# Interleaving the high and low parts of each weight tile in a three-pass float32r matmul kernel

## Chip, cores and metric

One core of one Trainium2 chip runs the whole program. The metric is the device time of one execution in microseconds (us), the median of several runs. The profile is of one execution of its own.

## What is computed

Two layers of a decoder trunk on 512 tokens of width 1024, in float32. Each layer has three sub-layers, each between two RMS norms and with a residual: a mixer (dilated attention heads and mLSTM heads), cross attention into 256 memory tokens, and a gated MLP. Cut to the dense products, which take nearly all of the time:

```
for l in range(DEPTH):                                     # 2
    proj  = rmsnorm(x, pre_mix_g[l]) @ w_in[l]             # 512x1024 @ 1024x3592
    x    += rmsnorm(concat(attn, mlstm) @ w_out[l], ...)   # @ 1024x1024
    q, k, v = rmsnorm(x, pre_mem_g[l]) @ wq, mem @ wk, mem @ wv
    x    += rmsnorm(softmax(q k / 16) v @ wo[l], ...)
    u     = causal_dwconv(rmsnorm(x, pre_ffn_g[l]) @ w_up[l], ...)   # @ 1024x5632
    a, g  = split(u)
    x    += rmsnorm((gelu(g) * a) @ w_down[l], ...)        # 512x2816 @ 2816x1024
```

## The kernel before

**Three products for one.** TensorE gets float32r operands, which keep fewer bits than float32. Each operand is therefore split into a high part (the value rounded to float32r) and a low part (the rest), and `mm3` (L113) issues three matmuls for one: high x high, high x low, low x high. `split` (L98) makes the parts: ACT writes the high part with a cast, DVE subtracts it from the source and writes the low part.

**Units of weights.** All weights lie in DRAM as 134 units per layer of 128 x 1024 values. `load_raw` (L84) brings one into a tile `raw` (two buffers, DMAs on SP's queue), `w_split` (L89) splits it into the tiles `whi` and `wlo` (five buffers each). Each of these has room for 1152 values per partition, of which 1024 are used from an offset of 0 or, with `HALF_OFF`, of 32 values (128 bytes).

**Who moves and who stands.** In a matmul one operand is loaded into the array (stationary, 128 columns) and the other streams through it (moving, up to 512 columns). In the names of the profile the first input is the moving one: pg<-whi,B moves a weight against a stationary activation, pg<-B,whi moves an activation against a stationary weight. `feat_gen` (L169) and `feat_halves` (L180) hold weights stationary, the first with 512 moving columns (or 256 for the memory tokens), the second with 256. `tok_gen` (L197) and `down` (L1218) move the weights, 512 columns at a time. B are tiles of activations, S and T tiles of the MLP's pool `forms`, mem the memory tokens.

**The up projection.** `up_products` (L1059) forms seven products of 256 moving columns for each pair of units j, from sums and differences of weight blocks and of activations. POOL builds the sums in tiles T (L1101 to L1104), `high` (L1111) casts on ACT and `low` (L1123) subtracts, on DVE for the kinds a, t and u (1024 values), on POOL for kind b (512 values, a tile of its own with 1120 values).

**Order.** PE's instructions stand in the order in which the program issues them, with side tasks woven in by a table of times (`PACE`, `tick`). In the up projection that holds for ACT, DVE, POOL and SP as well. Elsewhere a scheduler orders these four, from the tiles' dependences and buffers.

## Time and profile before

| | |
|---|---|
| median of 3 runs | 1577.69 us (1576.15 to 1578.36) |
| the profiled execution | 1576.06 us, of it the span 1574.3 us |
| PE busy (matmul) | 1547.4 us, 98% of the span, 9480 matmuls |
| PEld busy (weight load) | 1371.0 us, 87% |
| DVE busy | 1049.2 us, 67% |
| ACT busy | 892.0 us, 57% |
| POOL busy | 326.5 us, 21% |
| DMA | 173.13 MB, mean 110 GB/s |

Matmuls overlap: the busy time of one reaches from its start to its modelled end, and the next starts before that. How long a matmul holds the engine is therefore read from the distance of two starts, not from its busy time. A group's idle time is that of the engine just before its instructions.

### The profile page before, as it was taken

To read this page: it belongs to the slowest core of one execution; us is meant where nothing else is said; L and a number is where in the kernel's file an instruction comes from. 1 tells how busy PE (TensorE), PEld (TensorE's weight loads), DVE (VectorE), ACT (ScalarE), POOL (GpSimd) and SP (SyncE) were. 2 spreads that over 40 slices of the span, in tenths; PEclk is the share of its full clock that TensorE was granted. 3 is DMA by queue.
4 is the path that set the end of the run, shared out by engine and by line. 5 is a ranking of instruction groups with operands and counts; after the bars stand their busy time and mean duration, and the time that the engine had idled before them with its cause. 6 is when DMAs were issued, how large, how long until landed. Compare 5 with 4: busy or idle time off the path is not lost.

```text
span 1574.3 us, 24497 instructions
## 1 busy us (share of the span) xinstructions
PE 1547.4 (98%) x9480; PEld 1371.0 (87%) x9480; DVE 1049.2 (67%) x1808; ACT 892.0 (57%) x1578; POOL 326.5 (21%) x292
## 2 busy tenths in 40 slices
PE   7999999999999999999999999999999999999998
PEld 5788888998899999988887888889888899999886
DVE  5687646746597777763376886557566977777433
ACT  5677574545466666653257775745445666666321
POOL 0000110100026666600010002101000466663000
PEclk9999999999999999999999999999999999999999
DMA  5421244552242333332333223445411233332331
GB/s 177 129 94 62 92 137 153 155 187 94 68 136 95 108 108 108 108 121 94 108 95 107 94 74 94 137 144 161 161 54 42 96 108 108 108 114 82 127 102 58
DMA packets 55430, 173.13 MB, mean 110 GB/s; under 512 B 6801, under 2 KB 9617, under 8 KB 55314
## 3 DMA queue, kind: packets, MB, share of 16 engines
q1 hardware_dynamic: 55314, 171.57, 33.4%
q8 instruction: 74, 1.21, 0.3%
q14 instruction: 42, 0.34, 0.1%
HBM read 165.22 MB, written 6.33 MB: 109 GB/s over the span
## 4 chain that ended last, share of the span: by engine, by line
PE 82%; DVE 6%; DMA 5%; ACT 3%; issue 2%; POOL 1%; SPq 0%; POOLq 0%; DVEq 0%; ACTq 0%
PE pg L107 51%; PE pa L107 28%; PE pa L111 2%; DMA raw<-in_w_dram 2%; DVE wlo L100 1%; DMA raw<-in_memt_dram 1%; ACT whi L99 1%; DVE xg L256 1%; POOL sm L230 1%; ACT junk L235 1%; DVE x L369 1%; DMA raw<-dk 1%; DVE wlo L1126 1%; DMA raw<-dv 1%; DMA dk<-kf 0%
## 5 line engine op out<-in xcount | busy, mean ns | idle before, releaser
L107 PE MATMUL pg<-B,whi 128*128 128x256 f32 (+1 forms) x1800 | 420.7, 327 | 8.2 <-DVE ql L995 3.9
L100 DVE TENSOR_TENSOR wlo<-raw,whi 128x1024 fp32r<-128x1024 f32 x188 | 230.6, 1228 | 215.7 <-ACT whi L99 213.1
L99 ACT CAST whi<-raw 128x1024 fp32r<-128x1024 f32 x188 | 197.2, 1050 | 217.8 <-PE pg L107 139.7
L107 PEld LDWEIGHTS pg<-B,whi 128*128 128x128 f32 x1800 | 290.8, 189 | 28.3 <-DVE ql L995 4.3
L107 PE MATMUL pg<-whi,B 128*128 128x512 f32 x896 | 297.8, 399 | 0.0
L107 PE MATMUL pg<-B,wlo 128*128 128x256 f32 (+1 forms) x896 | 288.4, 322 | 0.0
L107 PEld LDWEIGHTS pg<-whi,B 128*128 128x128 f32 x896 | 168.6, 188 | 35.1 <-DVE B L100 1.3
L230 POOL TENSOR_TENSOR sm<-sm,mhalf 128x1 f32<-128x1 f32 x56 | 34.3, 612 | 724.2 <-DVE sm L355 548.3
L107 PEld LDWEIGHTS pg<-B,wlo 128*128 128x128 f32 x896 | 168.9, 188 | 13.6
L107 PE MATMUL pg<-wlo,B 128*128 128x512 f32 x448 | 175.3, 391 | 0.6 <-DVE sm L248 0.6
L107 PE MATMUL pa<-S,whi 128*128 128x256 f32 x960 | 175.5, 283 | 0.0
L1031 DVE SCALAR_TENSOR_TENSOR u<-pg,fcw,u 128x511 f32<-128x511 f32 (+1 forms) x176 | 131.3, 747 | 38.2 <-ACT u L1026 35.2
L107 PEld LDWEIGHTS pa<-S,whi 128*128 128x128 f32 x960 | 148.4, 190 | 0.0
L107 PE MATMUL pa<-S,wlo 128*128 128x256 f32 x480 | 135.6, 282 | 0.0
L1126 DVE TENSOR_TENSOR wlo<-T,whi 128x1024 fp32r<-128x1024 f32 x80 | 103.9, 1299 | 9.7 <-ACT whi L1120 9.7
L107 PE MATMUL pa<-whi,S 128*128 128x512 f32 x320 | 105.9, 390 | 0.0
L107 PE MATMUL pg<-whi,S 128*128 128x512 f32 x320 | 105.4, 390 | 0.0
L1120 ACT CAST whi<-T 128x1024 fp32r<-128x1024 f32 x80 | 83.5, 1044 | 32.9 <-PE pg L107 30.8
L1026 ACT ACTIVATE u<-pg,fcw 128x512 f32<-128x512 f32 x88 | 68.5, 779 | 57.2 <-PE pg L107 37.2
L107 PEld LDWEIGHTS pg<-wlo,B 128*128 128x128 f32 x448 | 84.7, 189 | 15.8 <-DVE wlo L100 1.0
L107 PEld LDWEIGHTS pa<-S,wlo 128*128 128x128 f32 x480 | 90.9, 189 | 0.0
L1126 POOL TENSOR_TENSOR b<-rg,b 128x512 fp32r<-128x512 f32 x40 | 51.6, 1290 | 142.7 <-ACT b L1120 142.7
(264 smaller groups left out, 2942.5 us busy)
## 6 DMA issues: line engine op xcount, KB each, us to landing
raw<-in_w_dram SPq DMA_DIRECT2D x228, 512.0 KB, 3.5
rg<-in_w_dram SPq DMA_DIRECT2D x40, 512.0 KB, 3.5
gain<-in_gains_dram SPq DMA_DIRECT2D x11, 512.0 KB, 4.0
raw<-in_memt_dram SPq DMA_DIRECT2D x20, 256.0 KB, 3.0
tb<-tb_d SPq DMA_DIRECT2D x16, 256.0 KB, 3.5
x<-in_x_dram SPq DMA_DIRECT2D x8, 256.0 KB, 5.6
e<-nmu_d SPq DMA_DIRECT2D x8, 256.0 KB, 3.7
dv<-vf SPq DMA_DIRECT2D x8, 256.0 KB, 4.4
```

What stands on the lines that cost most here:

```text
L99: ACT.copy(hi, src)
L100: DVE.tensor_sub(lo, src, hi.bitcast(F32))
L107: PE.matmul(o, lhs, rhs, **kw)
L111: PE.transpose(o, src, idn)
L230: POOL.tensor_tensor(r, v, mhalf[:, :1], ALU.pow)
L235: ACT.activation(junk[:, :src.shape[-1]], src, AF.Square, accum_out=s_)
L256: DVE.scalar_tensor_tensor(xg, xt[:, c], r, g[h], ALU.mult, ALU.mult)
L369: DVE.scalar_tensor_tensor(xs[t][:, cc], self.hg[hh, t], r, xs[t][:, cc], ALU.mult, ALU.add)
L1026: ACT.activation(u, acc, AF.Identity, bias=fcw_t[:, m, 3:4], scale=fcw_t[:, m, 2:3])
L1031: DVE.scalar_tensor_tensor(u[:, q:], acc[:, :512 - q], fcw_t[:, m, 2 - q:3 - q], u[:, q:], ALU.mult, ALU.add)
L1120: ACT.copy(ws[j, kind][0], source(j, kind))
L1126: sub(ws[j, kind][1], source(j, kind), ws[j, kind][0].bitcast(F32), ALU.subtract)
```

## The change

Each weight unit now has one tile `wi` of 128 x 1036 x 2 values in place of `whi` and `wlo`. Its high part is every even value, its low part every odd one, so two neighbouring columns of either part lie 8 bytes apart. The tile of kind b is interleaved in the same way, without offset. The 12 unused pairs make the pitch of the five buffers 8288 bytes, which is 16 x 512 + 96; the offsets `off` and `HALF_OFF` are gone. The pool of weights is 4640 bytes per partition smaller, and what is allocated after it lies that much lower. A reader of the names should know that whi, wlo and b's parts are all called wi or b in the changed kernel.

```diff
-    def w_split(raw, off=0):
-        hi = pp.tile([128, 1152], F32R, tag="whi", name=nm("whi"), bufs=5)[:, off:off + 1024]
-        lo = pp.tile([128, 1152], F32R, tag="wlo", name=nm("wlo"), bufs=5)[:, off:off + 1024]
+    def w_tile():
+        both = pp.tile([128, 1036, 2], F32R, tag="wi", name=nm("wi"), bufs=5)
+        return both[:, :1024, 0], both[:, :1024, 1]
+
+    def w_split(raw):
+        hi, lo = w_tile()
         split(raw, hi, lo)
         return hi, lo
 
-    def load_unit(l, i, off=0):
-        return w_split(load_raw(l, i), off)
+    def load_unit(l, i):
+        return w_split(load_raw(l, i))
...
-    HALF_OFF = 32
...
     def feat_halves(l, units, act, dones, between):
-        ws = [load_unit(l, u, HALF_OFF) for u in units]
+        ws = [load_unit(l, u) for u in units]
...
             if kind == "b":
-                t = forms.pool.tile([128, 1120], F32R, tag="b", name=nm("b"))
-                ws[j, kind] = t[:, 96:608], t[:, 608:1120]
+                t = forms.pool.tile([128, 512, 2], F32R, tag="b", name=nm("b"))
+                ws[j, kind] = t[:, :, 0], t[:, :, 1]
             else:
-                ws[j, kind] = [pp.tile([128, 1152], F32R, tag=tg, name=nm(tg), bufs=5)[:, HALF_OFF:HALF_OFF + 1024]
-                               for tg in ("whi", "wlo")]
+                ws[j, kind] = w_tile()
             ACT.copy(ws[j, kind][0], source(j, kind))
```

PE's and POOL's instructions keep their order. On ACT and DVE the scheduler puts 21 of the 308 casts of weights one to three places later, and the subtracts with them. One place on ACT, early in the first layer's mixer, where the casts of weights (raw is the source) stand among the casts of the attention's keys (kh). Before:

```order
L99 CAST whi_941<-raw_939 128x1024
L733 CAST kh_436<-pg_505 64x512
L734 CAST kh_436<-pg_505 64x512
L733 CAST kh_437<-pg_505 64x512
L734 CAST kh_437<-pg_505 64x512
L649 ACT_TABLE_LOAD
```

And with the change:

```order
L735 CAST kh_432<-pg_499 64x512
L736 CAST kh_432<-pg_499 64x512
L102 CAST wi_931<-raw_929 128x1024
L735 CAST kh_433<-pg_499 64x512
L736 CAST kh_433<-pg_499 64x512
L651 ACT_TABLE_LOAD
```

The cast of the weight moved behind the first two casts of keys. On DVE at the same place, where the weights' low parts stand among those of the queries (qa) and keys (kl). Before:

```order
L100 TENSOR_TENSOR wlo_808<-raw_805,whi_807 128x1024
L726 SCALAR_TENSOR_TENSOR qa_434<-pg_444,qa_434 64x512
L726 SCALAR_TENSOR_TENSOR qa_435<-pg_444,qa_435 64x512
L100 TENSOR_TENSOR wlo_942<-raw_939,whi_941 128x1024
L735 TENSOR_TENSOR kl_428<-pg_505,kh_436 64x512
L735 TENSOR_TENSOR kl_429<-pg_505,kh_437 64x512
```

And with the change:

```order
L728 SCALAR_TENSOR_TENSOR qa_430<-pg_439,qa_430 64x512
L103 TENSOR_TENSOR wi_798<-raw_796,wi_798 128x1024
L728 SCALAR_TENSOR_TENSOR qa_431<-pg_439,qa_431 64x512
L737 TENSOR_TENSOR kl_424<-pg_499,kh_432 64x512
L103 TENSOR_TENSOR wi_931<-raw_929,wi_931 128x1024
L737 TENSOR_TENSOR kl_425<-pg_499,kh_433 64x512
```

Both subtracts of weights moved by one place, behind the first of the two parts for queries and for keys.

## Rows read from the trace of the kernel before

**Rows 1.** The page, parts 1 and 2: busy time by engine, and slices of the span.
```profile
PE 1547.4 (98%) x9480; PEld 1371.0 (87%) x9480; DVE 1049.2 (67%) x1808; ACT 892.0 (57%) x1578; POOL 326.5 (21%) x292
...
PE   7999999999999999999999999999999999999998
...
PEclk9999999999999999999999999999999999999999
```

**Rows 2.** The page, part 4: the chain that ended last, by engine.
```profile
PE 82%; DVE 6%; DMA 5%; ACT 3%; issue 2%; POOL 1%; SPq 0%; POOLq 0%; DVEq 0%; ACTq 0%
```

**Rows 3.** Groups by shape, moving weights: out<-moving,stationary, shape, count | busy us, mean ns | idle.
```profile
L107 PE MATMUL pg<-whi,B 128*128 128x512 f32 x896 | 297.8, 399 | 0.0
...
L107 PE MATMUL pg<-wlo,B 128*128 128x512 f32 x448 | 175.3, 391 | 0.6 <-DVE sm L248 0.6
...
L107 PE MATMUL pa<-whi,S 128*128 128x512 f32 x320 | 105.9, 390 | 0.0
L107 PE MATMUL pg<-whi,S 128*128 128x512 f32 x320 | 105.4, 390 | 0.0
...
L107 PE MATMUL pa<-wlo,S 128*128 128x512 f32 x160 | 62.3, 389 | 0.0
L107 PE MATMUL pg<-wlo,S 128*128 128x512 f32 x160 | 62.2, 389 | 0.0
...
L107 PE MATMUL pg<-whi,mem 128*128 128x512 f32 x128 | 47.5, 414 | 0.0
...
L107 PE MATMUL pg<-wlo,mem 128*128 128x512 f32 x64 | 25.3, 395 | 0.0
...
L107 PE MATMUL pa<-whi,T 128*128 128x512 f32 x32 | 10.5, 390 | 0.0
```

**Rows 4.** Timeline of PE, down projection: start us, us, what, matmuls merged into the row.
```profile
750.02 0.61 PE L107 MATMUL pg<-whi,S 128*128 128x512 f32 x2
750.47 0.39 PE L107 MATMUL pg<-wlo,S 128*128 128x512 f32 x1
750.70 0.61 PE L107 MATMUL pg<-whi,S 128*128 128x512 f32 x2
751.15 0.39 PE L107 MATMUL pg<-wlo,S 128*128 128x512 f32 x1
751.38 0.39 PE L107 MATMUL pg<-whi,S 128*128 128x512 f32 x1
```

**Rows 5.** Timeline of PE, up projection: the same columns.
```profile
640.27 0.28 PE L107 MATMUL pa<-S,wlo 128*128 128x256 f32 x1
640.39 0.40 PE L107 MATMUL pa<-S,whi 128*128 128x256 f32 x2
640.63 0.28 PE L107 MATMUL pa<-S,wlo 128*128 128x256 f32 x1
640.75 0.40 PE L107 MATMUL pa<-S,whi 128*128 128x256 f32 x2
640.98 0.28 PE L107 MATMUL pa<-S,wlo 128*128 128x256 f32 x1
```

**Rows 6.** Groups by shape, stationary weights with 256 moving columns: first and last of eleven.
```profile
L107 PE MATMUL pg<-B,whi 128*128 128x256 f32 x1152 | 210.2, 282 | 1.3 <-ACT pg L1173 0.9 <-DVE B L277 0.4
...
L107 PE MATMUL pg<-S,wlo 128*128 128x256 f32 x32 | 9.1, 283 | 0.0
```

**Rows 7.** Groups by shape: casts and subtracts of 1024 and of 512 elements.
```profile
L100 DVE TENSOR_TENSOR wlo<-raw,whi 128x1024 fp32r<-128x1024 f32 x188 | 230.6, 1228 | 215.7 <-ACT whi L99 213.1 <-PE pa L107 2.2
...
L99 ACT CAST whi<-raw 128x1024 fp32r<-128x1024 f32 x188 | 197.2, 1050 | 217.8 <-PE pg L107 139.7 <-DMA raw<-in_w_dram 73.7 <-DVE wlo L100 1.3
...
L100 DVE TENSOR_TENSOR S<-B,S 128x512 fp32r<-128x512 f32 x28 | 19.1, 684 | 0.0
...
L99 ACT CAST S<-B 128x512 fp32r<-128x512 f32 x28 | 17.2, 616 | 0.0
```

**Rows 8.** Windows: from:to, us, each engine's busy us (x instructions), clock, DMA share, GB/s.
```profile
481.00:678.00 197.00, 196.01 (x1647) 195.54 (x1647) 154.94 (x198) 128.27 (x198) 119.07 (x93) 1.00 0.30 100
678.00:824.00 146.00, 145.55 (x667) 120.79 (x666) 73.55 (x110) 57.74 (x97) 5.45 (x10) 1.00 0.33 110
```

## The prediction

> **What bounds the kernel now.** I read the page's first two parts first: PE is busy for 98% of the span, nine tenths or more in every slice but the first and the last, at the full granted clock [rows 1]. The chain that ended last says the same: 82% of it is PE [rows 2]. So this is a kernel in which TensorE never waits for long, and a change of layout can act in two ways only: it changes how long one matmul holds TensorE, or it slows ACT, DVE or POOL so much that TensorE has to wait after all.

> A busy time does not give the pace, because matmuls overlap. For that I took the timeline of PE and looked at the starts alone. In the down projection, where weights are the moving operand of 512 columns, six matmuls start between 750.02 and 751.38 us: 0.227 us each [rows 4]. In the up projection, with 256 moving columns, six start between 640.27 and 640.98 us: 0.118 us each [rows 5]. The difference, 0.109 us for 256 columns, is 0.42 ns per column, so a 512-column matmul streams for about 0.216 us and has some 0.01 us around it. Those columns are 4 bytes wide: the moving stream sweeps along its tile at 4 / 0.42 = 9.5 bytes per ns.

> Then I sorted the matmuls by what the change does to them. In a name such as pg<-whi,B the first input is the moving one. Weights move in twelve groups, all 512 wide: the eight largest have 896 + 448 + 4 groups of S (320 + 320 + 160 + 160) + 128 + 64 = 2,496, and four groups against T add 32 + 32 + 16 + 16, together 2,592 [rows 3]. Weights stand still, with 256 moving columns, in eleven groups from 1,152 down to 32 matmuls, 4,512 in all [rows 6]. In both the new tile puts 8 bytes between neighbouring columns in place of 4.

> **The change part by part.**

> *Moving weights, 2,592 matmuls.* To read 512 columns the stream has to pass 4,096 bytes of the tile in place of 2,048. No trace row shows such a read, so I bound it. From below: the step costs nothing, 0.227 us stay, +0. From above: the stream passes no more than the 9.5 bytes per ns that it passes now; then the streamed part doubles, +0.216 us each. Which end is nearer? Look for the fastest reader in the profile. ACT's cast takes 1,050 ns for 1,024 elements and 616 for 512, so 0.85 ns per element; DVE's subtract takes 1,228 and 684, so 1.06 ns per element [rows 7]. These sweep 4.7 and 3.8 bytes per ns in an operand. The moving stream is already at twice the speed of any other reader, and the free end asks for 19 bytes per ns, twice the best that any row shows. I take the upper end: 2,592 x 0.216 = +560 us. Nothing covers it, for these matmuls stand back to back with 0.0 to 0.6 us of idle time per group [rows 3].

> [...]

> *Weights that stand still, 4,512 matmuls of 256 columns and 968 of 512.* A weight load fits into the 0.118 us between two starts now. With the new step it passes 1,024 bytes instead of 512, which is 8.7 bytes per ns, still under the 9.5 of the moving stream. So I take 0. Upper bound: if the load's pace halves, up to 0.236 us per matmul, 4,512 x 0.118 = +532 us; the 512-wide ones would hide it behind their 0.227. Lower bound: if loads and stream disturb each other less than now, down to the streamed 0.108 us: 4,512 x -0.010 = -45 us.

> *Addresses.* Before, all weight tiles lie at one address modulo 512 (whi and wlo have a pitch of 9 x 512 bytes), shifted by 128 bytes where they stand still behind 256 columns. Now the pitch is 8,288 = 16 x 512 + 96 bytes, so five tiles have five residues. What lies behind them in SBUF starts 4,640 bytes lower, which shifts S and T by 32 bytes modulo 512. The starts in both stretches are even to 10 ns, so I see no price for residues beyond the 0.01 us that is not streamed; I take 0, and -0.01 to +0.01 us per matmul, about 45 us either way, as bounds.

> *ACT, DVE and POOL.* The same instructions are issued: no matmul, cast or DMA more or less. The cast writes every second word and the subtract reads and writes every second word, 308 times each. At 1.06 ns per element a step of 8 bytes is a sweep of 7.5 bytes per ns, below the 9.5 of PE, so I take 0. If the pace per element doubled, DVE would need 1.09 us more per split. In the loop over up-projection units DVE is busy 154.9 of 197 us, ACT 128.3, POOL 119.1 [rows 8], for 19.6 iterations of 84 matmuls: DVE has 2.1 us to spare of each 10.05. Three splits per iteration would take 3.3. POOL's subtract of 512 elements once per iteration has 4 us to spare.

> *Order of ACT and DVE.* 21 of the 308 casts stand one to three places later, because one tile is free only when its low half has been read as well. A cast behind two casts of 64x512 waits about 1.2 us more; the weights are converted several units of some 5 us ahead, and PE idled 0.6 us at most in the groups above. I take 0; without that cover it would be 21 x 1.2 = 25 us.

> **Sum.** 1576.06 us (the profiled execution, 1.76 over its span, 1.6 under the median of the runs) + 560 = 2136 us. For this case alone I would give 2100 to 2250: from the bounds of residues and of order, and a part of the weight loads' price.

> **The rivals.**

> *The step is free and the streams stop disturbing each other: faster.* Weight load and 256-column stream would pass 1,024 bytes each in the same time, so they could run side by side without meeting, and the 0.118 us could fall towards 0.108. Place: the 4,512 matmuls of the stages where weights stand still. Price: up to -45 us, 1531; half of it, about 1553, is likelier. It decides only if the moving weights cost nothing: 2,592 matmuls at +0.017 us would eat it all. For it: PE alone sets the time, so every ns shows. Against it: the sweep speed above.

> *The step is free for PE and nothing else changes.* Then 1576, within 0.2%.

> *The step is free for PE but not for DVE: slower by little.* From the point at which a split costs 0.7 us more, DVE fills the 2.1 us of each up-projection iteration and PE waits for wlo; at the doubled pace 3.3 - 2.1 = 1.2 us x 40 iterations = +48 us, and latencies in other stages would add some: about 1625. [...]

> *Weight loads halve as well.* 2136 + 532 = 2668 us; for it speaks that the loads have hardly any time to spare between starts of 0.118 us, against it that they sweep at half the moving stream's speed now.

> **How the numbers follow.** Forecast 0.43; both streams halved 0.09; free for PE but not for DVE, or residues that cost, 0.17; free and nothing changes 0.06; faster 0.25. About 0.2% is what a measurement of this kernel can tell from no change. Slower is 0.43 + 0.09 + 0.17 = 0.69, same 0.06, faster 0.25. The likeliest case gives 2136 us. A range for 8 in 10 must reach down through the cases in which the step is free: from 1545, which leaves out less than half of the faster case, to 2250, which leaves out the case of both streams.

> **What would show it.** Right: in the down projection the starts stand about 0.44 us apart, in the up projection still 0.118; the stretch from 678 to 824 us grows to some 281 us (624 matmuls x 0.216 more than its 146), the one from 481 to 678 keeps its 197; ACT's cast stays near 1,050 ns and DVE's subtract near 1,228; PE stays at 98%. Wrong: starts of moving weights at 0.22 to 0.24 us refute the forecast outright. Starts of 0.11 us in the up projection would show the faster rival, DVE at 1.9 us per split with PE waiting for wlo the one of DVE, starts of 0.2 us and more in the up projection the halved loads. Between these, a pace of the moving weights near 0.3 us would say that the mechanism is right and the size is not.

## The result, and the profile after

The changed kernel takes 2156.49 us (median of four runs, 2155.05 to 2157.74), the kernel before 1576.92 us in the same comparison: ratio 1.3676, 95% interval 1.3652 to 1.3700. It is slower by 36.8%. The forecast was 2136 us, with a range of 2100 to 2250 if its own case held, and of 1545 to 2250 for 8 in 10 over all cases.

The page after, parts 1, 2 and 4, which answers to [rows 1] and [rows 2]:

```profile
span 2154.1 us, 24436 instructions
...
PE 2134.5 (99%) x9480; PEld 1436.7 (67%) x9480; DVE 1064.7 (49%) x1808; ACT 922.0 (43%) x1578; POOL 326.2 (15%) x292
...
PE   8999999999999999999999999999999999999998
...
PEclk9999999999999999999999999999999999999999
...
PE 96%; DVE 1%; issue 1%; ACT 1%; POOL 0%; DMA 0%; SPq 0%; DVEq 0%; POOLq 0%; ACTq 0%
```

The same 9480 matmuls at the same granted clock (mean 0.997 before, 0.999 after), and TensorE busy in every slice: it has not begun to wait for another engine. PE's idle time even fell, from 1574.3 - 1547.4 = 26.9 us to 2154.1 - 2134.5 = 19.6 us, and PE's part of the chain rose from 82% to 96%. So the 580 us lie inside the matmuls. The groups by shape with weights as the moving operand, which answer to [rows 3] (high and low part now have one name, so a group holds both):

```profile
L110 PE MATMUL pg<-wi,B 128*128 128x512 f32 x1344 | 627.6, 645 | 0.0
...
L110 PE MATMUL pa<-wi,S 128*128 128x512 f32 x480 | 226.3, 650 | 0.0
L110 PE MATMUL pg<-wi,S 128*128 128x512 f32 x480 | 225.7, 650 | 0.0
```

The first group was 297.8 + 175.3 = 473.1 us in its two parts, now 627.6 with 0.0 idle. These two can't be set against each other: the busy times of the high and the low part overlapped (a row of [rows 4] ends at 750.02 + 0.61 = 750.63, the next starts at 750.47), so that a part of the 473.1 is counted twice. The pace stands in PE's timeline of the down projection (start us, us, what, matmuls merged into the row), beside [rows 4]:

```profile
998.53 5.64 PE L110 MATMUL pg<-wi,S 128*128 128x512 f32 x12
1003.97 5.63 PE L110 MATMUL pa<-wi,S 128*128 128x512 f32 x12
1009.40 2.92 PE L110 MATMUL pg<-wi,S 128*128 128x512 f32 x6
```

A row merges matmuls into one output tile; from the start of a row of 12 to the start of the next are twelve starts. (1003.97 - 998.53) / 12 = 0.453 us, where it was 0.227: twice as much. In the up projection, where weights stand still, beside [rows 5]:

```profile
739.73 1.61 PE L110 MATMUL pa<-S,wi 128*128 128x256 f32 x12
741.18 1.60 PE L110 MATMUL pg<-B,wi 128*128 128x256 f32 x12
```

1.45 / 12 = 0.121 us, where it was 0.118. The windows of the two stretches, up projection and down projection of the first layer, answer to [rows 8]:

```profile
650.00:849.00 199.00, 198.83 (x1651) 198.45 (x1650) 156.90 (x196) 135.05 (x196) 120.88 (x93) 1.00 0.30 99
849.00:1135.00 286.00, 285.55 (x668) 133.66 (x668) 75.95 (x110) 59.99 (x97) 5.46 (x10) 1.00 0.18 58
```

The up projection takes 199 us in place of 197, the down projection 286 in place of 146. The casts and subtracts, beside [rows 7]:

```profile
L103 DVE TENSOR_TENSOR wi<-raw,wi 128x1024 fp32r<-128x1024 f32 x188 | 231.0, 1231 | 485.4 <-ACT wi L102 485.2
...
L102 ACT CAST wi<-raw 128x1024 fp32r<-128x1024 f32 x188 | 210.3, 1123 | 477.4 <-PE pg L110 404.9 <-DMA raw<-in_w_dram 45.2 <-issue 20.8
```

DVE's subtract kept its time (1231 ns, before 1228); ACT's cast takes 7% more (1123, before 1050), and ACT waits for PE most of the time (404.9 of the 477.4 us that it idled before these casts).

### The profile page after: what moved, and what is told of

Read it like the earlier page. It is cut to its first block, busy times and chain, and to the rows that moved or that the text cites. A ratio compares the mean times of both kernels' runs of the same rounds, so it can differ in the third digit from the quotient of the medians.

```text
span 2154.1 us, 24436 instructions
## 1 busy us (share of the span) xinstructions
PE 2134.5 (99%) x9480; PEld 1436.7 (67%) x9480; DVE 1064.7 (49%) x1808; ACT 922.0 (43%) x1578; POOL 326.2 (15%) x292
## 4 chain that ended last, share of the span: by engine, by line
PE 96%; DVE 1%; issue 1%; ACT 1%; POOL 0%; DMA 0%; SPq 0%; DVEq 0%; POOLq 0%; ACTq 0%
PE pg L110 67%; PE pa L110 26%; PE pa L114 2%; DVE wi L1127 0%; DMA raw<-in_w_dram 0%; DVE B L103 0%; ACT B L102 0%; DVE wi L103 0%; DVE S L103 0%; POOL T L1106 0%; ACT wi L1121 0%; DVE xg L258 0%; ACT wi L102 0%; ACT junk L237 0%; DVE u L1033 0%
## 5 line engine op out<-in xcount | busy, mean ns | idle before, releaser
L110 PE MATMUL pg<-wi,B 128*128 128x512 f32 x1344 | 627.6, 645 | 0.0
L110 PE MATMUL pg<-B,wi 128*128 128x256 f32 (+1 forms) x2696 | 478.3, 326 | 3.3 <-DVE u L1033 2.4
L103 DVE TENSOR_TENSOR wi<-raw,wi 128x1024 fp32r<-128x1024 f32 x188 | 231.0, 1231 | 485.4 <-ACT wi L102 485.2
L110 PEld LDWEIGHTS pg<-wi,B 128*128 128x128 f32 x1344 | 271.9, 207 | 289.2 <-issue 283.0
L110 PEld LDWEIGHTS pg<-B,wi 128*128 128x128 f32 x2696 | 394.3, 196 | 32.6 <-issue 2.2
L102 ACT CAST wi<-raw 128x1024 fp32r<-128x1024 f32 x188 | 210.3, 1123 | 477.4 <-PE pg L110 404.9
L110 PE MATMUL pa<-wi,S 128*128 128x512 f32 x480 | 226.3, 650 | 0.0
L110 PE MATMUL pg<-wi,S 128*128 128x512 f32 x480 | 225.7, 650 | 0.0
L110 PE MATMUL pa<-S,wi 128*128 128x256 f32 x1440 | 186.4, 283 | 0.0
L110 PEld LDWEIGHTS pa<-S,wi 128*128 128x128 f32 x1440 | 179.4, 196 | 0.1
L1127 DVE TENSOR_TENSOR wi<-T,wi 128x1024 fp32r<-128x1024 f32 x80 | 109.9, 1374 | 13.8 <-ACT wi L1121 13.8
L1127 POOL TENSOR_TENSOR b<-rg,b 128x512 fp32r<-128x512 f32 x40 | 58.4, 1459 | 142.8 <-ACT b L1121 142.8
```

The lines of the kernel that those rows point to most:

```text
L102: ACT.copy(hi, src)
L103: DVE.tensor_sub(lo, src, hi.bitcast(F32))
L110: PE.matmul(o, lhs, rhs, **kw)
L1127: sub(ws[j, kind][1], source(j, kind), ws[j, kind][0].bitcast(F32), ALU.subtract)
```

## The experiments

The place of the loss was plain from the trace; what was open is the rule. The prediction's theory says **bytes passed**: the moving stream sweeps no more than 9.5 bytes of tile per ns. A rival says **pieces**: the stream reads whole aligned pieces of 8 or 16 bytes and pays for each piece that it touches. The change also did four things at once: one tile for two, a step in moving weights, a step in standing ones, other addresses.

All kernels below put both parts of a unit in one tile w of 2304 words with five buffers, whose pitch keeps the address modulo 512 of the kernel before. Two constants set the layout of moving and of standing weights: None is contiguous, (n, r) takes runs of r words out of a pattern of n streams. The core of it:

```diff
+    MOVING, STANDING = None, None
+    def w_tile(lay, off=0):
+        t = pp.tile([128, 2304], F32R, tag="w", name=nm("w"), bufs=5)
+        if lay:
+            return parts(t[:, off:off + 2048], lay)
+        return Part(t[:, off:off + 1024], 1, 1), Part(t[:, 1152 + off:1152 + off + 1024], 1, 1)
...
-        hi, lo = load_unit(l, u)
+        hi, lo = load_unit(l, u, STANDING)
...
-                wu = load_unit(l, U_DOWN + k)
+                wu = load_unit(l, U_DOWN + k, MOVING)
```

**One tile, contiguous.** The edit above and nothing else.

> Control: both parts of a unit in one tile, high part first, low part behind it, contiguous, at the residues of the kernel before (pitch 18 x 512 bytes, HALF_OFF kept). My theory: the common tile and the few casts that it moves later cost nothing that can be measured, 1577 us, within 5. Rival (the coupling of the two parts' buffers delays the casts): up to 25 us more, 1600.

Measured: 1574.9 us, ratio 0.9992 (0.9979 to 1.0006). One tile in place of two, with its later casts, costs nothing; the runs that follow stand on this.

**Standing weights with a step of 8 bytes.**

```diff
-    MOVING, STANDING = None, None
+    MOVING, STANDING = None, (2, 1)
```

> Interleaved only where weights stand still (kind b too); moving weights stay contiguous. My theory: the whole loss is in the moving weights, so 1577 us plus what the starts of the changed kernel show for standing weights (0.120 to 0.121 us instead of 0.119 with 256 columns, 4,512 times; 0.232 instead of 0.228 with 512, 968 times), 8 to 12 us: about 1587. Rival (a weight load pays for the step too): starts of 0.2 us and more with 256 columns, 1950 us or more.

Measured: 1585.37 us, ratio 1.0059 (1.0036 to 1.0083). PE's timeline, up projection:

```profile
640.12 1.62 PE L151 MATMUL pa<-S,w 128*128 128x256 f32 x12
641.57 1.62 PE L151 MATMUL pa<-B,w 128*128 128x256 f32 x12
```

0.121 us per matmul, as in the changed kernel: 4,512 times some 0.002 to 0.003 us are the 9 us. A step of 8 bytes costs the weight loads next to nothing.

**Five residues modulo 512, contiguous.** The addresses of the changed kernel: five tiles at five addresses modulo 512 bytes (tile of 2072 words, low part at 1036, no HALF_OFF, kind b's tile without offset).

```diff
-        t = pp.tile([128, 2304], F32R, tag="w", name=nm("w"), bufs=5)
+        t = pp.tile([128, 2072], F32R, tag="w", name=nm("w"), bufs=5)
...
-    HALF_OFF = 32
+    HALF_OFF = 0
```

> The other half of the change alone: the parts stay contiguous, but the five tiles have the changed kernel's pitch of 16 x 512 + 96 bytes, no HALF_OFF, and what lies behind them moves down by 4,640 bytes. My theory: residues cost at most some ns per matmul, 1577 to 1600 us. Rival (the residues carry the loss, through reads of two operands that meet): 1900 us or more.

Measured: 1582.75 us, ratio 1.0044 (1.0031 to 1.0057). The moving matmuls are a little slower (12 in 2.79 us, 0.233 each):

```profile
750.42 2.95 PE L151 MATMUL pg<-w,S 128*128 128x512 f32 x12
753.21 1.08 PE L151 MATMUL pa<-w,S 128*128 128x512 f32 x4
```

So addresses have a price, of 7 us and not of hundreds. Summed over the whole trace and set against the control run, the distances from one start to the next grew by 11 us where weights move and fell by 4 us where they stand still behind 256 columns.

**Moving weights in runs of four words.** High and low part alternate every 16 bytes, so a stream of 512 columns passes 4,096 bytes, as in the changed kernel.

```diff
-    MOVING, STANDING = None, None
+    MOVING, STANDING = (2, 4), None
```

> Moving weights in runs of four words: four of the high part, four of the low part, in turn; a matmul still passes 4,096 bytes for 512 columns, but takes 16 of every 32 in one piece. Three theories of what the moving stream is limited by. Pieces of 16 bytes, fetched whole: each is used in full, starts stay at 0.227 us, 1577 us. Bytes passed, as my prediction had it: starts of 0.453 us, 2163 us. Pairs of words, fetched as 8 bytes: 0.227 us, 1577 us.

Measured: 1582.79 us, ratio 1.0041 (1.0026 to 1.0055). Timeline, down projection:

```profile
751.37 2.96 PE L151 MATMUL pg<-w,S 128*128 128x512 f32 x12
754.17 2.96 PE L151 MATMUL pa<-w,S 128*128 128x512 f32 x12
```

2.80 / 12 = 0.233 us with twice the bytes passed. The theory of bytes passed has fallen: 4,096 bytes in 0.233 us are 17.6 bytes per ns, where it allowed 9.5.

**Runs of two words, a step of 16 bytes, a step of 32 bytes.** Three runs for the size of a piece, 8 or 16 bytes. In the last two the columns of a unit are dealt to four or eight streams that lie word by word side by side.

```diff
-    MOVING, STANDING = None, None
+    MOVING, STANDING = (2, 2), None
...
+    MOVING, STANDING = (4, 1), None
...
+    MOVING, STANDING = (8, 1), None
```

> Moving weights in runs of two words, standing ones contiguous. Runs of four cost almost nothing, so the stream is not limited by the bytes that it passes over, but by the pieces that it fetches. [...] Rival, a piece has 8 bytes (two words): starts of 0.227 us, about 1583 us.

> Moving weights with 16 bytes between neighbouring columns: four streams (two halves of the high part, two of the low part) interleaved in one tile. Pieces of 16 bytes: one column per piece, 512 pieces instead of 128, starts of 4 x 0.227 = 0.907 us, 1577 + 2592 x 0.680 = 3340 us. Rival, pieces of 8 bytes: 512 pieces instead of 256, starts of 0.453 us, 2163 us.

> Moving weights with 32 bytes between neighbouring columns (eight streams; a matmul of 512 columns takes two of them, one after the other). It settles what is left of my prediction's wording, a limit on the bytes passed. If the stream pays per piece fetched, whatever lies between the pieces: no more than a step of 16 bytes costs, 3340 us with pieces of 16 bytes, 2163 with pieces of 8. If it pays for the way: twice the price of a step of 16 bytes, about 5700 us.

Measured: 2145.76 us (ratio 1.3620, 1.3566 to 1.3675), 2193.33 us (1.3922, 1.3869 to 1.3976) and 2122.81 us (1.3475, 1.3422 to 1.3527). Timelines of the down projection, one row of 12 and the next of each:

```profile
999.90 5.62 PE L151 MATMUL pa<-w,S 128*128 128x512 f32 x12
1005.34 2.90 PE L151 MATMUL pg<-w,S 128*128 128x512 f32 x6
```

```profile
999.90 5.72 PE L151 MATMUL pa<-w,S 128*128 128x512 f32 x12
1005.43 2.95 PE L151 MATMUL pg<-w,S 128*128 128x512 f32 x6
```

```profile
1001.03 5.35 PE L151 MATMUL pa<-w,S 128*128 128x512 f32 x12
1006.21 2.33 PE L151 MATMUL pg<-w,S 128*128 128x512 f32 x5
```

0.453, 0.461 and 0.432 us. Both sizes of piece have fallen as well: pieces of 8 bytes would have left the runs of two words at the full pace, pieces of 16 bytes, met by the runs of two words (half of each piece unused, 2 x 0.227 us), would have made each step of 16 bytes twice as dear as one of 8. In the runs so far there are two paces, about 0.23 and about 0.45, and nothing between or beyond.

**Standing weights with a step of 16 bytes.**

```diff
-    MOVING, STANDING = None, None
+    MOVING, STANDING = None, (4, 1)
```

> Standing weights with 16 bytes between columns, moving ones contiguous: does the weight load have the same limit? With pieces of 16 bytes at the pace of the moving stream (1.77 ns each), a load of 128 columns takes 128 pieces, 0.227 us, and can no longer hide behind 256 moving columns: starts of some 0.23 to 0.24 us instead of 0.119, 4512 x 0.115 = +520 us, 2100 us; behind 512 columns it still fits. With a step of 8 bytes it would take 64 pieces, 0.113 us, which just fits into 0.119, as the run with a step of 8 bytes showed (1585 us). Rival (loads have no such limit): about 1590 us.

Measured: 2125.67 us, ratio 1.3493 (1.3437 to 1.3549). Timeline of the up projection, and the group of casts there:

```profile
639.88 2.96 PE L151 MATMUL pg<-B,w 128*128 128x256 f32 x12
642.68 0.63 PE L151 MATMUL pg<-S,b 128*128 128x256 f32 x2
```

```profile
L1165 ACT CAST w<-T 128x1024 fp32r<-128x1024 f32 x80 | 164.4, 2055 | 89.2 <-PE pg L151 89.2
```

0.233 us per matmul, twice the 0.118: 4,512 x 0.115 = 519 of the 550 us. Most of the rest, 27 us in the sum of the distances between starts, lies at the 968 matmuls of 512 columns. The writers are slow as well: the cast takes 2055 ns here and 1044 in the kernel before. But PE hardly waits for them. Its idle time is 2122.6 - 2088.8 = 33.8 us, 6.9 more than before, and no weight tile is in the list of its waits:

```profile
PE 2088.8 (98%) x9480; PEld 1949.3 (92%) x9480; DVE 1212.9 (57%) x1808; ACT 1106.9 (52%) x1578; POOL 338.7 (16%) x292
```

So the load sets the pace. The groups of loads of one name in the control run, with a step of 8 bytes and with one of 16:

```profile
L151 PEld LDWEIGHTS pa<-S,w 128*128 128x128 f32 x1440 | 176.5, 188 | 0.0
```

```profile
L151 PEld LDWEIGHTS pa<-S,w 128*128 128x128 f32 x1440 | 181.8, 197 | 0.0
```

```profile
L151 PEld LDWEIGHTS pa<-S,w 128*128 128x128 f32 x1440 | 346.1, 331 | 0.0
```

A load takes 188, 197 and 331 ns. A weight load has a limit too, but it lies at one step more than that of the moving stream: 8 bytes are nearly free, 16 are not. What kind of limit this is, these runs do not show. A load passes 1,024 bytes of the tile at a step of 8 and 2,048 at a step of 16; 2,048 in 0.233 us are 8.8 bytes per ns, so the prediction's limit on the bytes passed fits the loads too. A step of 32 bytes for standing weights would tell the two apart; it was not run. The moving stream, at half its pace (0.453 us) already at 8 bytes, behaves as if its own step were twice what the access says. That gave a new theory, **two readers**: the columns of the moving stream are dealt in turn to two readers, and a reader keeps its pace if it meets each 16-byte line of the tile at least twice. Contiguous columns, or aligned runs of four, give each reader two words of a line; every other layout so far gives it one. Both the readers and the 16 bytes of a line are assumptions of the theory; what speaks for them so far is aligned runs of four words at 0.233 us and runs of two at 0.453. The runs below test them. The rival that is left: the full pace wants four neighbouring words one behind the other in the access, wherever they lie.

**Columns dealt to two regions, and runs of four across lines.** In the first two runs each block of 512 columns lies as two regions of 256 contiguous words, even columns in one and odd ones in the other, 1024 or 1152 bytes apart. No two columns that follow each other are neighbours, but each of two readers would walk along one region. The third shifts the runs of four by 8 bytes, so that each lies across two lines.

```diff
+    class Dealt:
...
+        def __getitem__(self, key):
+            k = key[1].start // 512
+            return self.v[:, k].rearrange("p s c -> p c s")
...
+            v = t[:, :8 * lay].rearrange("p (s c) -> p s c", s=8)
+            return Dealt(v[:, :4, :256]), Dealt(v[:, 4:, :256])
...
-            return parts(t[:, off:off + 2048], lay)
+            return parts(t[:, off + 2:off + 2050], lay)
```

> Each block of 512 moving weight columns lies as two regions of 256 contiguous words, the even columns in one and the odd ones in the other, 1024 bytes apart; the moving access alternates between the regions. Standing weights and everything on PE else are as in the kernel before; ACT and DVE read raw with a step of 8 bytes and write contiguous words. Theory of two readers (the stream is dealt column by column to two readers, and a reader keeps the full pace as long as it meets each 16-byte line of the tile at least twice): every reader meets a line four times, so the pace stays at 0.227 us per 512 columns or falls a little: 1577 us, at the lowest 2592 x -0.011 = 1549 us. Rival (the full pace wants four neighbouring words one behind the other in the access): no two columns one behind the other are neighbours, so the pace halves, 0.43 to 0.46 us: 2120 to 2190 us.

> As the run with regions 1024 bytes apart, but with 1152 bytes between the two regions, so that the two readers never stand at the same address modulo 512. Theory of two readers: 1549 to 1577 us, as there; if the two differ by more than 0.3%, the address modulo 512 of the two readers matters. Rival (four neighbouring words): 2120 to 2190 us.

> The layout of the run with runs of four words, shifted by 8 bytes: a run of four neighbouring columns now spans two 16-byte lines and has half of each. Theory of two readers: each of them meets a line only once, so the pace halves, about 0.453 us per 512 columns: about 2163 us. Rival (a run of four neighbouring words in the access is enough, wherever it lies): 0.233 us as in the run without the shift, about 1583 us.

Measured: 1565.01 us (ratio 0.9941, 0.9922 to 0.9959), 1557.53 us (0.9879, 0.9851 to 0.9908) and 2153.52 us (1.3662, 1.3616 to 1.3707). Timelines of the regions 1024 and 1152 bytes apart and of the shifted runs:

```profile
752.06 2.75 PE L166 MATMUL pg<-w,S 128*128 128x512 f32 x12
754.65 2.54 PE L166 MATMUL pa<-w,S 128*128 128x512 f32 x11
```

```profile
749.88 2.75 PE L166 MATMUL pg<-w,S 128*128 128x512 f32 x12
752.47 1.89 PE L166 MATMUL pa<-w,S 128*128 128x512 f32 x8
```

```profile
1000.85 5.64 PE L151 MATMUL pa<-w,S 128*128 128x512 f32 x12
1006.31 4.27 PE L151 MATMUL pg<-w,S 128*128 128x512 f32 x9
```

2.59 / 12 = 0.216 us for both distances of the regions and 5.46 / 12 = 0.455 us for the shifted runs. The theory of two readers met all three, and the rival fell on all three: columns that are no neighbours run at full pace, and four neighbours at a wrong address at half of it. Dealt regions are even faster than contiguous columns (0.227 us), in both runs. The two differ by 0.5%, more than the 0.3% that the expectation took as a sign that the readers' addresses matter. But the pace of the moving matmuls is the same in both; what differs is the engines that write: the cast takes 1261 ns with 1024 bytes between the regions and 1107 with 1152 (first and second row), and DVE's subtract 1347 and 1229:

```profile
L158 ACT CAST w<-raw 128x1024 fp32r<-128x1024 f32 x188 | 236.7, 1261 | 178.3 <-PE pg L166 88.5 <-DMA raw<-in_w_dram 80.7 <-DVE w L159 3.5
```

```profile
L158 ACT CAST w<-raw 128x1024 fp32r<-128x1024 f32 x188 | 207.7, 1107 | 198.6 <-PE pg L166 106.2 <-DMA raw<-in_w_dram 85.4 <-issue 2.3
```

Of 2,592 x 0.011 = 28.5 us the better run keeps 17.6 in its span (1556.7, against 1574.3 before): PE's idle time grew from 26.9 to 1556.7 - 1521.0 = 35.7 us:

```profile
PE 1521.0 (98%) x9480; PEld 1375.0 (88%) x9480; DVE 1053.8 (68%) x1808; ACT 901.4 (58%) x1578; POOL 331.4 (21%) x292
```

**High and low part in shared lines, in another order.** The test of the change itself: both parts share every 16-byte line again and the stream passes 8 bytes per column, as in the changed kernel, but a line holds columns 0 and 2 of both parts, the next one columns 1 and 3.

```diff
+    class Shared:
...
+        def __getitem__(self, key):
+            return self.v[:, key[1].start // 4:key[1].stop // 4].rearrange("p m b a -> p m a b")
...
+            v = t[:, off:off + 2048].rearrange("p (m b s a) -> p s m b a", b=2, s=2, a=2)
+            return Shared(v[:, 0]), Shared(v[:, 1])
```

> Both parts of a moving weight again share every 16-byte line, and the stream passes as many bytes of the tile as in the changed kernel (8 per column); only the order in the lines differs. One line holds the high values of columns 0 and 2 and the low values of columns 0 and 2, the next those of columns 1 and 3, and so on. Standing weights are contiguous as before. Theory of two readers (columns dealt in turn, two hits on a line keep the pace): the first reader meets the first line with columns 0 and 2, the second the next line with columns 1 and 3, two hits each, so 0.216 to 0.233 us per 512 columns, 1549 to 1583 us. Rival (the line must not be shared with the other part, or the bytes passed count after all): 0.44 to 0.46 us, 2130 to 2190 us. ACT writes runs of two words, as in the run with runs of two: 1050 to 1100 ns.

Measured: 1577.94 us, ratio 1.0021 (1.0011 to 1.0031).

```profile
749.96 2.92 PE L165 MATMUL pg<-w,S 128*128 128x512 f32 x12
752.72 1.54 PE L165 MATMUL pa<-w,S 128*128 128x512 f32 x6
```

2.76 / 12 = 0.230 us. Sharing lines with the other part costs nearly nothing (contiguous columns took 0.227). ACT's cast takes 1103 ns, just over the 1050 to 1100 expected. So the changed kernel loses its 580 us not because the two parts share lines, but by which columns of one part share a line.

## Why the prediction was right, and where its reason was wrong

**What bounds the kernel.** Right: PE sets the time before and after, and the change acts only through the length of a matmul.

**Moving weights, +560 us.** The direction, the place and nearly the size were right. The term was mis-sized: 0.453 - 0.227 = 0.226 us, not 0.216, so 2,592 x 0.226 = 586 us. The step that failed is the division of 0.227 us into 0.216 that are streamed and "some 0.01 us around it" that stay: all of it doubled, and the dealt regions, at 0.216, suggest that the 0.01 us were a loss of the stream itself and no fixed cost. With 586 the sum is 2162 us, against 2156 measured. Summed over all matmuls of the two traces, the distances from one start to the next grew by 577 us where weights move (603 to 1180) and by 3 us everywhere else together, against 2154.1 - 1574.3 = 579.8 of the spans. Of the 9 us between 586 and 577, PE's idle time, which fell by 7.3, can account for most.

**The reason given for it.** Wrong. "The stream passes no more than the 9.5 bytes per ns that it passes now" gave the right number for a step of 8 bytes because a halved pace and a doubled path are the same number there. That the time was met is luck in this sense. The range of 1545 to 2250, from a faster kernel to far above the forecast, says little by holding, and the prediction itself gave its case 0.43. Runs of four words pass 17.6 bytes per ns, a step of 32 bytes passes 16,384 in 0.432 us, 38 per ns. The comparison with ACT and DVE as slower readers therefore decides nothing. A rule that fits all ten layouts of moving weights (contiguous, a step of 8 bytes in the changed kernel, and eight more in the runs) is two hits on a 16-byte line for each of two readers (0.216 to 0.233 us where the layout gives them, 0.432 to 0.461 where it does not); four of the ten were run after it was formed, and all four came as it said. That two readers exist as hardware is an inference; no row shows them one by one. The same ten fit without them: the pace is full where each column shares its line with the column two places before or behind it.

**Standing weights, 0.** Right within 0.003 us per matmul: in the changed kernel the distances behind the 4,512 matmuls sum to 548.1 us, before to 548.4, and the run with standing weights alone gives +0.6%. The bound of +532 us, a halved load, turns up one step later, at 16 bytes (0.233 us per matmul, after 0.121 at 8). Whether sweep speed, the reason given, is the limit here stays open without a step of 32 bytes.

**Addresses, 0 within 45 us either way.** The run with the five residues alone costs 7 us, 0.4%: inside the bounds, and not nothing.

**ACT, DVE and POOL, 0.** Right for the time: PE's waits for weight tiles come to 1.4 us, before to 2.2. DVE's 1231 ns refute the rival "free for PE but not for DVE" in its second half: the up projection's subtracts took 1284 and 1374 ns, before 1283 and 1299, so the step of 8 bytes cost DVE at most 0.08 us per split, not the 0.7 us at which that rival begins to count. With a step of 16 bytes DVE takes 1754 ns in the run that moves such weights. ACT's 7% more was not foreseen; ACT waits for PE, so it costs nothing. Nor was POOL's: its subtract of kind b takes 1459 ns, before 1290, well within the 4 us that it had to spare.

**Order, 0.** Right: the control run, with one tile per unit, gives 0.9992.

**The rivals.** Both free-step rivals fell with the pace of 0.453 us, and the halved loads with 0.121. The signs that the prediction named came in: starts 0.44 us apart (0.453), the down projection at 281 us (286), the up projection at 197 (199), PE at 98% (99%); only ACT's cast left its 1,050 ns.

## What to carry to other kernels

## What was not expected of the hardware

- Contiguous columns are not the fastest layout of the moving operand here. With even and odd columns in regions 1152 bytes apart, 512 columns take 0.216 us in place of 0.227, and the kernel takes 1557.53 us, 0.9879 of the kernel before (0.9851 to 0.9908): it beats both kernels. Why two regions help, and lines 16 bytes apart (0.230) do not, stays open.
- The half pace is not one number: 0.461 us at a step of 16 bytes, 0.453 at 8 and 0.432 at 32. These are about twice the full paces 0.230, 0.227 and 0.216 seen in other layouts. No run here tells why.
- A line has nearly one price wherever the pace is halved. This is an estimate under the theory of two readers: each of them meets 256 lines in 0.432 to 0.461 us, 1.69 to 1.80 ns per line, and a weight load with a step of 16 bytes meets 128 lines in 0.233 us, 1.82 ns per line.
- Where ACT and DVE fill the four regions of a part in one instruction, one behind the other, a distance of 1024 bytes costs them 154 and 118 ns per split over one of 1152, although the words that they write then lie without a gap. Whether PE's reads of the regions or their own writes are the cause was not tried.
